# Forward substitution on GpSimd for the inverses of the 16x16 diagonal blocks

## The chip, the cores and the metric

The kernel runs on one core of one Trainium2 chip. The metric is the device time of one execution in microseconds (us); the median of several runs is compared.

## The reference

One block of a hybrid encoder on 256 frames of width 2048: a Mamba-2 SSD mixer and an RWKV-7 time mixer read the same normed input through one input projection, their outputs go through one output projection, and a SwiGLU feed-forward layer and a final norm follow. The part that matters here is the recurrence of the RWKV-7 mixer, over 32 heads of 64 channels:

```python
def step(S, inp):
    r_t, w_t, k_t, v_t, a_t, b_t = inp
    sa = jnp.einsum('bhvk,bhk->bhv', S, a_t)
    S = S * w_t[:, :, None, :] + sa[..., None] * b_t[:, :, None, :] + v_t[..., None] * k_t[:, :, None, :]
    return S, jnp.einsum('bhvk,bhk->bhv', S, r_t)
```

The kernel evaluates it in chunks of 64 frames. Within a chunk the vectors `sa` of its frames depend on each other through a triangular matrix with ones on its diagonal, so each chunk and head needs the inverse of one 64x64 unit triangular matrix.

## The kernel before

**Stages.** The work is a long row of weight products on TensorE. The weights are read in 512 KB pieces into `raw` (four buffers, issued by SyncE, whose queue is in order). Each piece is split into a high part `whi` by ScalarE (line 192) and a rest `wlo` by VectorE (line 193), four buffers each, and goes into three matmuls per tile: lines 277 to 279 in `gemm_a` (256 columns wide), lines 298 to 300 in `gemm_b` (512 wide). First comes the input projection of the RWKV columns, in eight windows of one pair of 128-channel blocks each (`ps_rkv`; four heads of 64 channels per window). Then come the columns of the SSD mixer (`ps_bc`, `ps_xs`, `ps_z`), the output projection in between (`ps_o`), and the feed-forward layer (`ps_gt`, `ps_up`, `ps_o`).

**Side work by ticks.** Each `gemm_a` or `gemm_b` calls `side.tick()` after every piece of weights. `Side` is a heap of functions with due times in ticks, counted from the start of a window; a function is called, and its instructions are emitted, at the first tick that is not before its due time. `window(pi, ticks)` fills the heap: `PREP` for pair pi, `AMATS` and `INV` for pair pi-1, `CHAIN` for pair pi-2. Windows 0 to 2 have 12 ticks (the 12 pieces of k, v and r), the others 16 (four more of the output projection), window 8 has 20 (the SSD's B and C columns). In windows of 12 ticks the due times of `INV` and `CHAIN` are scaled by 11.5/16. The compiler's order on each engine is fixed before the run. It is near the order of emission but not the same: in the trace, instructions of one chain on VectorE stand between those of others, and loads of weights that were emitted later stand ahead of an earlier transfer that is not yet ready.

**The inverse of one pair** (8 chunk slots of two heads each, so 16 matrices of 64x64, each with four 16x16 diagonal blocks, 64 small blocks in all):

- `inv_out` (lines 597 to 611) picks the diagonal blocks out of `atb` into `dg` on VectorE, sends them to DRAM (`sc_n`, line 604) and reads them back as `nb` (line 606), 64 partitions, one 16x16 block per partition, on SyncE's queue. GpSimd fills `xb` with unit matrices (lines 609 and 610).
- `inv_level(s)` for s = 1, 2, 4, 8 (lines 613 to 656) inverts the blocks in each partition by doubling: from inverses of size s to those of size 2s by two products X21 = X22 N21 X11. All of it is on VectorE: one copy (line 628), then ten products (line 650) and ten sums along the last axis (line 652).
- `inv_in` (lines 658 to 668) sends `xb` to DRAM (`sc_X`, line 660), reads it back as `cm` in the layout of 128 partitions (line 663), and makes `X` (line 666) and its transpose `XT` on VectorE.
- `lev16a`, `lev16b`, `lev32a`, `lev32b` (lines 684 to 717) go from 16 to 32 and 64 by small TensorE products `ps_b` (line 677), with steps on VectorE and ScalarE between them. The result `XF` is read by the chain of the next window (`step_r`, line 737).

`nb`, `xb`, `dg`, `X` and `XT` have one buffer each.

Of the kernel before, what the change touches and what calls it, by code (L numbers as in the profile page):

```python
# [13 lines left out]
ALU = mybir.AluOpType  # L14
AX = mybir.AxisListType
# [17 lines left out]

PREP = (1.081, 1.2, 4.2, 5.2, 5.536, 6.756, 8.05, 9.2)
AMATS = (0.132, 1.4, 2.027, 2.231, 2.69, 3.323, 6.493)
INV = (5.002, 6.276, 7.732, 9.62, 9.939, 11.691, 11.849, 12.652, 15.9)
STEPS = (0.667, 2.0, 5.0)
SSD = (0.9, 2.7, 4.842, 6.642, 8.442, 8.924, 10.724, 12.524, 12.657, 16.124)
CHAIN = (0.05, 1.043, 2.306, 3.569, 4.833, 5.933, 7.196, 8.459, 9.08, 11.159, 12.747, 13.38)
# [29 lines left out]
def tile_hybrid_block(ctx: ExitStack, tc: tile.TileContext, x, norm1_g, w_in, conv_w, conv_b, dt_bias, A_log, D_skip,  # L69
                      ssd_norm_g, mu, w0, w2, a0, a2, g2, k_k, k_a, r_k, gn_w, gn_b, w_out, norm2_g, w_gate, w_up,  # L70
                      w_down, norm_f_g, out):
    nc = tc.nc
    PS = bass.MemoryType.PSUM
    x = x[0]
    out = out[0]
# [10 lines left out]
    side = Side()  # L86
# [7 lines left out]
    def bc(ap, n):  # L94
        return ap.unsqueeze(ap.ndim).broadcast_to(list(ap.shape) + [n])
# [3 lines left out]
    xv = x.rearrange("(b p) d -> p b d", p=P)  # L99
# [52 lines left out]
    for hh in range(2):  # L152
        for s in range(2):
            m = mask2[hh * 64:(hh + 1) * 64, s]
# [4 lines left out]
    for s in range(2):  # L159
        for hh in range(2):  # L160
            a = hh * 64
# [48 lines left out]
    def finish(i, b):  # L210
        r = rstd[i][:, b:b + 1]
        nc.vector.tensor_reduce(r, ssq[i][:, b], axis=AX.X, op=ALU.add)
        nc.scalar.activation(r, r, AF.Sqrt, bias=eps6, scale=1.0 / D)
        nc.vector.reciprocal(r, r)
        return r
# [221 lines left out]
    def rwkv_pair(pi, st):  # L437
        cb0 = 2 * pi

        def tl(name, shape=(P, 2, T), bufs=1, tag=None):  # L440
            return rp.tile(list(shape), F32, name=name, tag=tag or name, bufs=bufs)
# [134 lines left out]
        def amat(name, key, half):  # L576
            def f():
                if half == 0:
                    st[name] = tl(name, (P, NCH, 2, 64), 2)
                dst = st[name]  # L580
                src = ch(st[key])
                ps = mxt("ps_a").rearrange("p (c t) -> p c t", c=4)
                for c in range(4):
                    for hh in range(2):
                        nc.tensor.matmul(hd(ps, hh)[:, c], hd(src, hh)[:, half * 4 + c],
                                         hd(st["ar"], hh)[:, half * 4 + c].rearrange("p a t -> p (a t)"),
                                         start=True, stop=True)
                nc.vector.tensor_tensor(dst[:, half * 4:half * 4 + 4].rearrange("p c a t -> p c (a t)"), ps,
                                        mask2.rearrange("p a t -> p (a t)").unsqueeze(1).broadcast_to([P, 4, P]),
                                        ALU.mult)  # L590
                if name == "atb":
                    d = dst[:, half * 4:half * 4 + 4, 0]
                    nc.vector.tensor_tensor(d, d, bc(st["nn"][:, half * 4:half * 4 + 4], 64), ALU.mult)
            return f


        def inv_out():
            tm = tl("t1", (P, NCH, 4, 16), 2)
            nc.vector.tensor_tensor(tm, st["atb"][:, :, 0].rearrange("p c (b t) -> p c b t", t=16),
                                    bc(bmask, 16).unsqueeze(1).broadcast_to([P, NCH, 4, 16]), ALU.mult)  # L600
            dg = tl("dg", (P, NCH, 16))
            nc.vector.tensor_reduce(dg, tm.rearrange("p c b t -> p c t b"), axis=AX.X, op=ALU.add)
            sc = dram.tile([NCH, P, 16], F32, name="sc_n")
            nc.sync.dma_start(out=sc.rearrange("c p t -> p c t"), in_=dg)
            nb = tl("nb", (64, 272))
            nc.sync.dma_start(out=nb[:, :256].rearrange("p (i t) -> p i t", t=16),
                              in_=sc.rearrange("c (x i) t -> (c x) i t", i=16))
            xb = tl("xb", (64, 272))
            nc.gpsimd.memset(xb, 0.0)
            nc.gpsimd.memset(xb[:, 0:256:17], 1.0)  # L610
            st["nb"], st["xb"] = nb, xb

        def inv_level(s):
            def f():
                nb, xb = st["nb"], st["xb"]
                nm = 8 // s

                def blocks(t, at, swap):

                    v = t[:, :nm * 34 * s].rearrange("p (m x) -> p m x", m=nm)[:, :, at:at + 16 * s]  # L620
                    v = v.rearrange("p m (j t) -> p m j t", t=16)[:, :, :, 0:s]
                    return v.rearrange("p m j t -> p m t j") if swap else v


                n21 = blocks(nb, s, False)
                x11 = blocks(xb, 0, True)
                if s == 1:
                    nc.vector.tensor_copy(blocks(xb, 16, False), n21)
                    return
                x22 = blocks(xb, 17 * s, False)  # L630
                x21 = blocks(xb, 16 * s, False)
                tt = tl("tt", (64, 64), 2)

                if s == 2:
                    cut = [(slice(0, nm), r) for r in range(s)]
                    shp = [64, nm, s, s]
                    tv = tt[:, :nm * s * s].rearrange("p (r m c) -> p m r c", r=s, c=s)
                else:
                    cut = [(m, slice(0, s)) for m in range(nm)]
                    shp = [64, s, s, s]  # L640
                    tv = tt[:, :nm * s * s].rearrange("p (m r c) -> p m r c", r=s, c=s)
                tj = tv.rearrange("p m j c -> p m c j")

                def product(out, a, b):

                    for m, r in cut:
                        pd = tl("pd", (64, 512), 2, tag="t1")
                        pv = pd[:, :shp[1] * s * s].rearrange("p (a c j) -> p a c j", c=s, j=s)
                        bb = b[:, m] if s == 2 else b[:, m].unsqueeze(1)
                        nc.vector.tensor_tensor(pv, a[:, m, r].unsqueeze(2).broadcast_to(shp), bb.broadcast_to(shp),  # L650
                                                ALU.mult)
                        nc.vector.tensor_reduce(out[:, m, r], pv, axis=AX.X, op=ALU.add)

                product(tv, n21.rearrange("p m j r -> p m r j"), x11)
                product(x21, x22, tj)
            return f

        def inv_in():
# [150 lines left out]
        def final():  # L809
# [3 lines left out]
            for j in range(2):  # L813
                for kk in range(2):
# [8 lines left out]
            nc.vector.tensor_tensor(yl, yo, yh.bitcast(F32), ALU.subtract)  # L823

        amats = [recept, sums, amat("atb", "bt", 0), amat("atb", "bt", 1), inv_out, amat("atk", "kt", 0),
                 amat("atk", "kt", 1)]
        inv = [inv_level(1), inv_level(2), inv_level(4), inv_level(8), inv_in, lev16a, lev16b, lev32a, lev32b]
        chain = [load2]
        for c in range(4):
            chain += [step_r(c), step_s(c)]  # L830
# [6 lines left out]
    def window(pi, ticks):  # L837
        if pi < 8:
            w = pairs[pi]
            w["load"]()  # L840
            for t, n in zip(PREP, ("decay", "rate", "keys", "keys2", "keysum", "btt", "vt", "ktt")):
                side.at(t, w[n])
        if 0 < pi < 9:
            w = pairs[pi - 1]
            for t, f in zip(AMATS, w["amats"]):
                side.at(t, f)
            for t, f in zip(INV, w["inv"]):
                side.at(t if ticks >= 16 else t * (ticks - 0.5) / 16, f)
        if pi > 1:
            for t, f in zip(CHAIN, pairs[pi - 2]["chain"]):  # L850
                side.at(t if ticks >= 16 else t * (ticks - 0.5) / 16, f)
# [5 lines left out]
    for pi in range(8):  # L857
        st = {}
        pairs.append(rwkv_pair(pi, st))
        window(pi, 16 if pi > 2 else 12)  # L860
        for i, (n, c) in enumerate((("k", CK), ("v", CV), ("r", CR))):
            ps = scaled(gemm_a(w_in, [(0, 256, c + pi * 256)], "ps_rkv"))
            t = pp.tile([P, 2, T], F32, name="rkv", tag="t" + n, bufs=1)
            for j in range(2):
                m = ((c - CR) // P) + 2 * pi + j
                shift(t[:, j], ps[:, j], omA[:, m:m + 1], colA[:, MU + m:MU + m + 1])
            st[n] = t
        out_rwkv(pi - 3)
        side.drain()


    window(8, 20)
    xzst = ExitStack()

# [6 lines left out]
    for i in range(4):  # L881
# [6 lines left out]
        for j in range(2):  # L888
            b = 2 * i + j
            conv(BC[:, b // 4, b % 4], ps[:, j], 16 + b)  # L890
    nc.scalar.activation(BC, BC, AF.Silu)
    out_rwkv(5)
    side.drain()
    window(9, 18)

    def ssd_group(g, xc, zs):
# [105 lines left out]
    for g in range(4):  # L1002
        xc = []
        for i in range(2):
            ps = scaled(gemm_a(w_in, [(0, 256, CXBC + g * 512 + i * 256)], "ps_xs"))
            t = xz.tile([P, 2, T], F32, name="xc", tag=f"xc{i}")
# [55 lines left out]
    for j in range(D_FF // 512):  # L1062
        c = j * 512
# [28 lines left out]
    for b in range(2):  # L1092
        s = slice(b * P, (b + 1) * P)
        for n, (hi, lo) in enumerate(ws):
# [5 lines left out]
            c = slice(n * 512, (n + 1) * 512)  # L1100
# [6 lines left out]
    for b in range(2):  # L1107
        r = finish(2, b)
        for n in (2, 3, 0, 1):
            c = slice(n * 512, (n + 1) * 512)  # L1110
            t = hg[b][n]
# [33 lines left out]
```

## Time and profile before

| what | value |
| --- | --- |
| median of 3 runs | 1673.48 us (1672.79 to 1674.52) |
| the profiled execution's own time | 1674.88 us |
| its span, first to last instruction | 1673.2 us |
| mean granted TensorE clock | 0.999 of full speed |
| busy: TensorE, weight loads, VectorE, ScalarE, GpSimd | 99%, 86%, 71%, 53%, 1% |

PE is TensorE, PEld its weight loads, DVE VectorE, ACT ScalarE, POOL GpSimd, SP SyncE; a q behind the name is the engine's sequencer or queue. In a row of instructions stand the line of the kernel, the engine, the operation, the tiles written and read (`out<-in`), their shapes and a count. In a timeline the first number is the start in us from the span's beginning, the second the length of the row, and the bracket behind it the idle time of the engine before it and who ended it. In the list of waits stand the total in us, the number of times and the longest.

### The profile page before, as it was taken

The page shows a single profiled execution, that of the slowest core. Times are in us where ns is not written, and L with a number is a line of the kernel's source. Part 1 is how long each engine was busy: PE and PEld are TensorE (multiplying, and loading weights), DVE is VectorE, ACT ScalarE, POOL GpSimd, SP SyncE. Part 2 cuts the span into 40 slices and gives each one's busy share as a digit, 9 for nine tenths or more (in the row PEclk, how much of TensorE's full clock was granted, in tenths as well). Part 3 has the DMA queues.
Part 4 walks back from the last instruction along what each step waited for, and adds up shares of the span by engine and source line. Part 5 has one row for each costly group of instructions (what it writes and reads, how often), then busy time and mean ns, then how long its engine had stood idle before and what let it go on. Part 6 is the DMA issues. An engine that isn't in the chain of part 4 may idle for free.

```text
span 1673.2 us, 30550 instructions
## 1 busy us (share of the span) xinstructions
PE 1654.7 (99%) x12386; PEld 1440.8 (86%) x12386; DVE 1196.1 (71%) x1859; ACT 892.7 (53%) x1390; POOL 18.0 (1%) x57
## 2 busy tenths in 40 slices
PE   8999999999999999999999999999999999999997
PEld 8999989899898998998988888888888888888886
DVE  7898889888888867978777746465565564554657
ACT  6655765765656456667565644444444444444444
POOL 3000000000000000000000000000000000000000
PEclk9999999999999999999999999999999999999999
DMA  8654445545455455665654666666666666666663
GB/s 256 173 147 117 131 127 147 145 121 148 119 150 146 121 171 182 204 209 157 177 171 152 204 192 190 194 190 189 191 190 197 186 193 191 189 189 197 190 190 126
DMA packets 212685, 286.91 MB, mean 171 GB/s; under 512 B 34978, under 2 KB 117696, under 8 KB 211904
## 3 DMA queue, kind: packets, MB, share of 16 engines
q1 hardware_dynamic: 211216, 282.67, 57.9%
q8 instruction: 97, 1.59, 0.4%
q0 software_dynamic: 752, 1.24, 0.3%
q10 hardware_dynamic: 576, 1.05, 0.2%
q14 instruction: 44, 0.36, 0.1%
HBM read 281.75 MB, written 3.18 MB: 170 GB/s over the span
## 4 chain that ended last, share of the span: by engine, by line
PE 73%; DVE 1%; DMA 0%; ACT 0%; issue 0%; DVEq 0%; SPq 0%
PE ps_o L298 8%; PE ps_o L300 7%; PE ps_o L299 7%; PE ps_gt L300 5%; PE ps_gt L298 5%; PE ps_up L299 5%; PE ps_gt L299 5%; PE ps_up L300 5%; PE ps_up L298 5%; PE ps_xs L277 2%; PE ps_xs L279 2%; PE ps_xs L278 2%; PE ps_z L300 2%; PE ps_z L299 2%; PE ps_z L298 2%; PE ps_bc L277 1%
## 5 line engine op out<-in xcount | busy, mean ns | idle before, releaser
L193 DVE TENSOR_TENSOR wlo<-raw,whi 128x1024 fp32r<-128x1024 f32 x508 | 620.2, 1221 | 373.9 <-ACT whi L192 372.2
L192 ACT CAST whi<-raw 128x1024 fp32r<-128x1024 f32 x508 | 532.9, 1050 | 623.5 <-PE ps_o L300 150.7
L277 PE MATMUL ps_rkv<-uh,whi 128*128 128x256 f32 x768 | 224.5, 292 | 0.0
L279 PE MATMUL ps_rkv<-uh,wlo 128*128 128x256 f32 x768 | 218.5, 285 | 0.7 <-DVE wlo L193 0.7
L278 PE MATMUL ps_rkv<-ul,whi 128*128 128x256 f32 x768 | 218.3, 284 | 0.0
L277 PEld LDWEIGHTS ps_rkv<-uh,whi 128*128 128x128 f32 x768 | 146.7, 191 | 5.5 <-issue 1.4
L279 PEld LDWEIGHTS ps_rkv<-uh,wlo 128*128 128x128 f32 x768 | 146.8, 191 | 1.7 <-DVE wlo L193 0.9
L278 PEld LDWEIGHTS ps_rkv<-ul,whi 128*128 128x128 f32 x768 | 146.8, 191 | 0.6
L298 PE MATMUL ps_gt<-whi,uh 128*128 128x512 f32 x352 | 137.1, 390 | 0.0
L299 PE MATMUL ps_gt<-wlo,uh 128*128 128x512 f32 x352 | 137.0, 389 | 0.0
L300 PE MATMUL ps_gt<-whi,ul 128*128 128x512 f32 x352 | 137.0, 389 | 0.0
L298 PE MATMUL ps_up<-whi,uh 128*128 128x512 f32 x352 | 136.9, 389 | 0.0
L299 PE MATMUL ps_up<-wlo,uh 128*128 128x512 f32 x352 | 136.9, 389 | 0.0
L300 PE MATMUL ps_up<-whi,ul 128*128 128x512 f32 x352 | 136.9, 389 | 0.0
L298 PE MATMUL ps_o<-whi,ah 128*128 128x512 f32 x336 | 131.7, 392 | 0.0
L300 PE MATMUL ps_o<-whi,al 128*128 128x512 f32 x336 | 130.9, 390 | 0.0
L299 PE MATMUL ps_o<-wlo,ah 128*128 128x512 f32 x336 | 130.7, 389 | 0.0
L311 DVE TENSOR_TENSOR h<-ps_o,h 128x512 f32<-128x512 f32 x184 | 120.0, 682 | 2.6 <-PE ps_o L300 2.2
L298 PE MATMUL ps_o<-whi,yh 128*128 128x512 f32 x256 | 105.7, 415 | 0.0
L299 PE MATMUL ps_o<-wlo,yh 128*128 128x512 f32 x256 | 100.2, 392 | 0.0
L300 PE MATMUL ps_o<-whi,yl 128*128 128x512 f32 x256 | 99.8, 394 | 0.0
L298 PEld LDWEIGHTS ps_up<-whi,uh 128*128 128x128 f32 x352 | 66.1, 188 | 13.7
(335 smaller groups left out, 3014.7 us busy)
## 6 DMA issues: line engine op xcount, KB each, us to landing
raw<-in_w_in_dram SPq DMA_DIRECT2D x180, 512.0 KB, 3.8
raw<-in_w_gate_dram SPq DMA_DIRECT2D x88, 512.0 KB, 3.8
raw<-in_w_up_dram SPq DMA_DIRECT2D x88, 512.0 KB, 3.7
raw<-in_w_down_dram SPq DMA_DIRECT2D x88, 512.0 KB, 4.6
raw<-in_w_out_dram SPq DMA_DIRECT2D x64, 512.0 KB, 4.4
csb<-cs_d SPq DMA_DIRECT2D x4, 1024.0 KB, 6.9
h<-in_x_dram SPq DMA_DIRECT2D x4, 512.0 KB, 7.5
g2s<-in_rwkv_g_dram SPq DMA_DIRECT2D x8, 256.0 KB, 3.5
```

The lines of the kernel that those rows point to most:

```text
L192: order(nc.scalar.copy(hi, raw))
L193: order(nc.vector.tensor_tensor(lo, raw, hi.bitcast(F32), ALU.subtract))
L277: nc.tensor.matmul(o, wh, uh[:, kt], start=first and b == 0, stop=False)
L278: nc.tensor.matmul(o, wh, ul[:, kt], start=False, stop=False)
L279: nc.tensor.matmul(o, wl, uh[:, kt], start=False, stop=last and b == 1)
L298: nc.tensor.matmul(ps[b], ah[:, s], hi[:, k], start=first, stop=False)
L299: nc.tensor.matmul(ps[b], ah[:, s], lo[:, k], start=False, stop=False)
L300: nc.tensor.matmul(ps[b], al[:, s], hi[:, k], start=False, stop=last)
L311: nc.vector.tensor_tensor(d, ps[b], d, ALU.add)
```

## The change

The four levels of doubling on VectorE go. In their place stands one function `inv_rows`, which inverts all 64 blocks by forward substitution on GpSimd: row i of the block, multiplied by the rows that are done, is added to all rows below it. Row 0 is a copy, rows 1 to 14 are a product and an addition each, 29 instructions of 64 partitions. All of them are handed out at due time 3.9. The send-back `inv_in` stays at 9.939, the levels behind it move. Windows of 12 ticks get a list of their own, `INV12`, where before the one list was scaled. `nb` and `xb` lose 16 unused columns, the scratch tile `pd` becomes 64x64 with a name of its own, `tt` goes.

```diff
-INV = (5.002, 6.276, 7.732, 9.62, 9.939, 11.691, 11.849, 12.652, 15.9)
+INV = (3.9, 9.939, 11.691, 12.3, 13.3, 15.9)
+INV12 = (3.9, 8.4, 9.9, 10.2, 10.9, 11.5)
...
-            nb = tl("nb", (64, 272))
+            nb = tl("nb", (64, 256))
...
-            xb = tl("xb", (64, 272))
+            xb = tl("xb", (64, 256))
...
-        def inv_level(s):
...
-                product(tv, n21.rearrange("p m j r -> p m r j"), x11)
-                product(x21, x22, tj)
+        def inv_rows(i0, i1):
+
+            def f():
+                nv = st["nb"][:, :256].rearrange("p (i t) -> p i t", t=16)
+                xv = st["xb"][:, :256].rearrange("p (t c) -> p t c", c=16)
+                for i in range(i0, i1):
+                    n, m = 15 - i, i + 1
+                    below = xv[:, m:, 0:m]
+                    if i == 0:
+                        nc.gpsimd.tensor_copy(below, nv[:, 0, 1:].unsqueeze(2))
+                        continue
+                    shp = [64, n, m]
+                    pd = tl("pd", (64, 64), 2)[:, :n * m].rearrange("p (t c) -> p t c", c=m)
+                    nc.gpsimd.tensor_tensor(pd, bc(nv[:, i, m:], m), xv[:, i, 0:m].unsqueeze(1).broadcast_to(shp),
+                                            ALU.mult)
+                    nc.gpsimd.tensor_tensor(below, below, pd, ALU.add)
             return f
...
-        inv = [inv_level(1), inv_level(2), inv_level(4), inv_level(8), inv_in, lev16a, lev16b, lev32a, lev32b]
+        inv = [inv_rows(0, 15), inv_in, lev16a, lev16b, lev32a, lev32b]
...
-            for t, f in zip(INV, w["inv"]):
-                side.at(t if ticks >= 16 else t * (ticks - 0.5) / 16, f)
+            for t, f in zip(INV if ticks >= 16 else INV12, w["inv"]):
+                side.at(t, f)
```

More of the change, by code (lines that the diff above doesn't have):

```diff
@@ L611, in inv_out @@
             st["nb"], st["xb"] = nb, xb
-        def inv_level(s):
+        def inv_rows(i0, i1):
             def f():
[L615 to L652, printed above, removed]
-                product(tv, n21.rearrange("p m j r -> p m r j"), x11)
-                product(x21, x22, tj)
```

## The prediction

> **What bounds the kernel now.** I read the page's busy shares and the chain that ended last, then the windows by stage, then what TensorE waited for, and last the timelines around one pair's inverse.
>
> ```profile
> span 1673.2 us, 30550 instructions
> PE 1654.7 (99%) x12386; PEld 1440.8 (86%) x12386; DVE 1196.1 (71%) x1859; ACT 892.7 (53%) x1390; POOL 18.0 (1%) x57
> PE 73%; DVE 1%; DMA 0%; ACT 0%; issue 0%; DVEq 0%; SPq 0%
> ```
> ```profile
> 0.00:650.00 650.00, 640.79 (x7493) 588.73 (x7494) 556.12 (x1065) 394.34 (x792) 17.46 (x56) 1.00 0.53 147
> 650.00:1673.00 1023.00, 1013.94 (x4895) 852.07 (x4893) 640.03 (x795) 498.36 (x599) 0.54 (x1) 1.00 0.62 187
> ```
>
> TensorE (PE) is busy 99% of the span and is nearly all of the chain. The columns of the windows are length, then busy time of PE, PEld, DVE, ACT and POOL, then the granted clock. The change lives in the first 650 us, where the eight RWKV pairs are worked. There VectorE (DVE) is busy 556.12 of 650 us, 86%, and GpSimd (POOL) 17.46, but TensorE still lacks only 650.00 - 640.79 = 9.2 us. A busy engine that is late shows as a wait of the one that needs it, so the waits of PE say what a lighter VectorE can return:
>
> ```profile
> PE ps_w L737 <- ACT rs L733: 1.8, 2, 1.0
> PE ps_R L225 <- DVE diag_r L224: 1.7, 1, 1.7
> PE ps_n L247 <- DMA h<-in_x_dram: 1.6, 1, 1.6
> PE ps_up L114 <- DVE eps L105: 1.1, 1, 1.1
> PE ps_b L677 <- DVE t1s L690: 0.8, 1, 0.8
> PE ps_b L677 <- DVE X L666: 0.8, 2, 0.4
> PE ps_rkv L279 <- DVE wlo L193: 0.7, 1, 0.7
> PE ps_dt L396 <- DVE dt_c L377: 0.6, 1, 0.6
> ```
>
> These eight are 9.1 us, the whole lack. Four belong to the start (L225, L247, L114, L396, 5.0 us), which the change does not touch. The four that can be touched are 1.8 + 0.8 + 0.8 + 0.7 = 4.1 us, 0.25% of the span. That caps what faster supply of TensorE can give.
>
> **What is removed.** Per pair, one copy and twenty small VectorE instructions (products L650, sums L652) leave.
>
> ```profile
> 0.00:650.00 650.00, 45.00 (x160) 1.00 0.53 147
> L628 DVE COPY xb<-nb x8: 155/168/169, 99.0 to 546.8; 64x8 f32<-64x8 f32 x8
> ```
>
> The first row is the first 650 us with the instructions on tile pd alone: 160 of them, 45.00 us of VectorE. With 8 copies of 0.168 us that is 46.3 us, 5.8 us per pair. On VectorE that is a saving; on TensorE it is worth only the waits above. I credit the 0.8 us of X (below: in the two short windows the send-back and its consumer are re-timed) and the 0.8 us of t1s. The other 2.5 us I leave: the ps_w waits end on ScalarE, and the wlo wait is a single one. Sum so far -1.6 us.
>
> **What is added on GpSimd.** Row 0 is one copy, rows 1 to 14 a product and an addition each: 29 instructions per pair, of (15-i)(i+1) elements per partition, 15 to 64 and 665 over the 14 rows, so 47.5 on average, each depending on the one before. No two-input GpSimd instruction is in this trace. The nearest rows:
>
> ```profile
> 12.31 1.04 POOL L148 TENSOR_SCALAR_AFFINE_SELECT trimask<-trimask 128x128 f32<-128x128 f32 x1
> 13.31 1.38 POOL L155 TENSOR_SCALAR_AFFINE_SELECT mask<-mask 64x64 f32<-64x64 f32 x4
> ...
> 113.32 0.32 POOL L609 MEMSET xb<- 64x272 f32 x1 [32.01 <-DVE wlo L193]
> 113.69 0.12 POOL L610 MEMSET xb<- 64x16 f32 x1
> ```
>
> Nearest in size and kind (reads, writes, 64 elements) is L155: four in 1.38 us, 0.345 us each. Between two dependent memsets lie 113.69 - 113.32 - 0.32 = 0.05 us. I take 0.40 us per instruction, a chain of 29 x 0.40 = 11.6 us. Ends: as cheap as the 64x16 memset, 0.17 each, 4.9 us; as dear as the 128-element select, 1.09 each, 31.6 us. POOL has nothing else to do in that time.
>
> [...] No row here shows a two-input GpSimd instruction.
>
> **How long the chain may be.** A late chain meets three others in turn. One is SyncE's (SP's) queue, which sends xb back in order (L660) with the weight loads behind it. The second is VectorE's order, in which X (L666) stands ahead of weight splits (wlo, L193). The third is TensorE's order, where ps_b (L677) stands between weight matmuls. The seventh pair, in a full window, rows of four engines in order of time:
>
> ```profile
> 475.62 0.48 SPq L606 DMA_DIRECT2D nb<-sc_n  x1
> 478.89 0.17 DVE L628 COPY xb<-nb 64x8 f32<-64x8 f32 x1 [0.24 <-DMA nb<-sc_n]
> 483.34 8.08 SPq L290 DMA_DIRECT2D raw<-in_w_out_dram  x3
> 493.30 0.64 DVE L652 TENSOR_REDUCE xb<-pd 64x64 f32<-64x512 f32 x1
> 494.01 0.49 SPq L660 DMA_DIRECT2D sc_X<-xb  x1
> 496.39 0.47 SPq L663 DMA_DIRECT2D cm<-sc_X  x1
> 500.70 0.43 DVE L666 TENSOR_TENSOR X<-cm,pmask 128x256 f32<-128x256 f32 x1
> 502.04 1.21 DVE L193 TENSOR_TENSOR wlo<-raw,whi 128x1024 fp32r<-128x1024 f32 x1
> 505.43 0.28 PE L278 MATMUL ps_rkv<-ul,whi 128*128 128x256 f32 x1
> 505.55 0.28 PE L279 MATMUL ps_rkv<-uh,wlo 128*128 128x256 f32 x1
> 505.76 0.22 PE L677 MATMUL ps_b<-X,atb 32*32 32x32 f32 x2
> ```
> ```profile
> SPq L660 <- DVE xb L652: 18.6, 8, 2.9
> ```
>
> The chain starts at 478.89 and ends at 493.94, 15.05 us, most of it VectorE's other work in between. SP is free at 491.42 and already waits for it, 2.3 us a pair on average (18.6 over 8) without harm: the loads behind it fill raw buffers that are needed later. X is done at 501.13 and TensorE reads it at 505.76, 4.6 us later. So a GpSimd chain of 11.6 us is 3.4 us early; SP would wait from 12.5 us; the ps_b on TensorE waits from 15.05 + 4.63 = 19.7 us. That is 0.68 us per instruction. The weight splits behind X on VectorE have cover of their own: with four buffers each of raw, whi and wlo they run ticks ahead of TensorE.
>
> The other end is the first inverse, in a window of 12 ticks:
>
> ```profile
> 98.99 0.17 DVE L628 COPY xb<-nb 64x8 f32<-64x8 f32 x1
> 110.51 0.66 DVE L652 TENSOR_REDUCE xb<-pd 64x64 f32<-64x512 f32 x1
> 117.86 0.43 DVE L666 TENSOR_TENSOR X<-cm,pmask 128x256 f32<-128x256 f32 x1 [0.49 <-DMA cm<-sc_X]
> 118.43 0.54 PE L677 MATMUL ps_b<-X,atb 32*32 32x32 f32 x23 [0.39 <-DVE X L666]
> ```
>
> The chain took 111.17 - 98.99 = 12.2 us with no slack at TensorE. Here the change re-times the steps: the old list was scaled by 11.5/16, which put inv_in at 7.14 and lev16a at 8.40 (ticks 8 and 9); INV12 has 8.4 and 9.9 (ticks 9 and 10), a tick later. A tick of gemm_a is 24 matmuls at 505.55 - 505.43 = 0.12 us, so at least 2.9 us. The budget becomes 12.2 + 0.1 + 2.9 = 15.2 us or more, 0.52 us per instruction. The chain of 11.6 fits, and the 0.8 us of waits for X (these two windows) goes.
>
> **What is moved, priced at nothing.** The send-back and its return are the same two DMAs in the same queue, the round trip unchanged. lev16b goes from tick 12 to 13 and lev32a from 13 to 14 in full windows; lev32b stays at 16. In the short windows lev16b and lev32a now fall into one tick (10.2 and 10.9, tick 11), which has to hold the addition to XT and its transposition between them; if nothing hides these, TensorE waits for two VectorE steps of X's size, 0.43 us each, 0.9 us a window in two windows. The new steps can split or merge groups of side matmuls. One group costs the entry 505.76 - 505.55 against 0.12, plus as much on leaving, about 0.2 us; one more or less in each of eight windows is 1.6 us, of either sign. That both signs are open is why I take zero.
>
> **Sum.** -1.6 us on the profiled span of 1673.2 us; that execution took 1674.88 us, the median of the three timed runs is 1673.48. On the median: 1671.9 us, -0.1%. A change under 0.2%, 3.3 us, I call none, about what this kernel's measurement can tell.
>
> **Rival: GpSimd too slow, TensorE waits (slower).** One mechanism: each GpSimd instruction takes over the budget. At 0.70 us the chain is 20.3 us. In the five full windows TensorE loses 20.3 - 19.7 = 0.6 us each, in the two short ones 5.1 each, and the last window taken like a full one. Sum 13.8 us, less the 1.6: 1685.7 us. It decides from 0.52 us per instruction. What could bring it there are VectorE's long two-input instructions:
>
> ```profile
> L193 DVE TENSOR_TENSOR wlo<-raw,whi 128x1024 fp32r<-128x1024 f32 x161 | 195.5, 1215 | 19.3 <-ACT whi L192 18.0
> ```
>
> wlo runs 195.5 of the 650 us, 30%. If each GpSimd read that meets one waits out half of 1.215 us, that adds 0.30 x 0.61 = 0.18 us, 0.58 each and 16.8 us in all: within the full windows' 19.7, 1.6 us over in the two short ones, so 1673.48 - 1.6 + 3.2 = 1675.1, no change still. If every one waits so, 1.01 each, 29.3 us: 9.6 x 6 + 14.1 x 2 = 85.8 us, 1757.7. [...] Chance of slower, all together, 0.19.
>
> **Rival: the lighter VectorE pays fully (faster).** All 4.1 us of waits go, and side groups merge, one less per window: 4.1 + 1.6 = 5.7 us, 1667.8 us. For it speaks the 86% of VectorE; against it that two of the waits end on ScalarE. Chance 0.16.
>
> **Rival: nothing changes because SP still waits.** With the chain at 15 us the SP wait stays as it was and only the waits for X go: 1672.7. It falls within no change, whose chance is 0.65 together.
>
> **How the numbers follow.** Forecast 1671.9; its own range, one group per window and the waits either way, 1669.5 to 1675.5. Toward slower the range reaches to 1682.0, past the shared-read case and most of the way to 0.70 us; below 1669.5 and above 1682.0 I leave about 0.08 and 0.11. Faster 0.16, same 0.65, slower 0.19.
>
> **What would show it.** VectorE down about 46 us in the first 650 us, GpSimd up by 29 instructions a pair, start to start near 0.4 us; sc_X issued no later after nb lands than 15 us; no wait of PE for X; PE idle in that stretch between 5 and 9 us. I am wrong if start to start on GpSimd exceeds 0.52 us and PE waits for X in most windows, or if the wlo instructions get visibly longer than 1.215 us while GpSimd runs.

## The result and the profile after

The changed kernel took 1756.78 us (median of 4 runs, 1752.63 to 1760.03) against 1673.81 us before (median of 4 runs, 1672.79 to 1674.52): ratio 1.0495, 95% interval 1.0471 to 1.0519. The forecast was no change. The profiled execution took 1752.63 us. Its page, span and busy shares:

```profile
span 1750.9 us, 30571 instructions
PE 1674.9 (96%) x12386; PEld 1459.6 (83%) x12386; DVE 1158.2 (66%) x1691; ACT 891.6 (51%) x1390; POOL 103.5 (6%) x289
```

The span is 77.7 us longer. TensorE's idle time went from 1673.2 - 1654.7 = 18.5 us to 1750.9 - 1674.9 = 76.0 us, 57.5 us more, and its busy time rose by 20.2 us although it executes the same 12386 matmuls. The first part is named by what TensorE waited for:

```profile
PE ps_r L705 <- DVE sn L736: 36.0, 6, 6.6
PE ps_rkv L280 <- DVE wlo L194: 7.8, 4, 2.2
PE ps_b L652 <- ACT Y L772: 6.0, 1, 6.0
PE ps_b L652 <- DVE X L641: 5.9, 1, 5.9
PE ps_b L652 <- DVE X L646: 1.8, 2, 1.3
PE ps_bc L280 <- DVE wlo L194: 1.7, 1, 1.7
```

The rows of `sn`, `wlo` and `ps_b` are 36.0 + 9.5 + 13.7 = 59.2 us; before, waits of these kinds were 0 + 0.7 + 1.6 us. The largest is new: six waits of about 6 us for `sn`, the running state of the recurrence, which the change does not touch (`step_s` of the pair one earlier; in this kernel lines 735 and 736, before 760 and 761). The timeline of the seventh pair, VectorE (DVE) and TensorE (PE) in order of time, shows why:

```profile
475.08 0.33 PE L701 MATMUL ps_r<-vt,atk 64*64 64x64 f32 x4
...
479.07 0.43 DVE L641 TENSOR_TENSOR X<-cm,pmask 128x256 f32<-128x256 f32 x1 [8.84 <-DMA cm<-sc_X]
479.53 0.45 DVE L646 STREAM_TRANSPOSE XT<-X 128x256 f32<-128x256 f32 x1
479.90 0.67 DVE L232 TENSOR_TENSOR ps_rkv<-ps_rkv,R 128x512 f32<-128x512 f32 x1
480.48 0.69 DVE L562 STREAM_TRANSPOSE btt<-bt 128x512 f32<-128x512 f32 x1
481.09 0.25 DVE L735 TENSOR_TENSOR sn<-ps_s,sn 128x128 f32<-128x128 f32 x1
...
481.65 0.28 DVE L736 TENSOR_TENSOR sn<-sn,pt 128x128 f32<-128x128 f32 x1
...
481.98 0.48 PE L705 MATMUL ps_r<-sn,ar 64*64 64x64 f32 x4 [6.57 <-DVE sn L736]
```

`X` waits 8.84 us for `cm`, and VectorE runs nothing else in that time. Behind `X` stand its own transposition, a scaling, another transposition and `sn`; on TensorE the matmul that reads `sn` is next in its order, and it stands still for 6.57 us. In the kernel before, the same two instructions began 8 to 9 us ahead of `X`, which began at 500.70:

```profile
491.71 0.25 DVE L760 TENSOR_TENSOR sn<-ps_s,sn 128x128 f32<-128x128 f32 x1
492.48 0.27 DVE L761 TENSOR_TENSOR sn<-sn,pt 128x128 f32<-128x128 f32 x1
```

So `X` has moved forward in VectorE's fixed order, past `sn`. Two rows of the stretch from 80 to 660 us add up what stood still beside TensorE: VectorE's eight waits for `cm`, and the waits of SyncE (SP) for the result of GpSimd (POOL):

```profile
DVE X L641 <- DMA cm<-sc_X: 67.9, 8, 9.1
```
```profile
SPq L635 <- POOL xb L630: 87.3, 8, 12.5
```

The 20.2 us of extra busy time come with a lower granted clock. Windows of this kernel around that stall (length, then busy time of PE, PEld, DVE, ACT and POOL, then the granted clock, the DMA engines' share and GB/s):

```profile
475.00:481.90 6.90, 0.42 (x6) 0.20 (x4) 2.79 (x8) 1.26 (x4) 0.42 (x2) 0.75 0.61 162
481.90:488.50 6.60, 6.42 (x41) 5.90 (x42) 4.17 (x7) 2.56 (x6) 0.00 (x0) 0.50 0.44 120
488.50:495.00 6.50, 6.50 (x71) 6.30 (x70) 2.50 (x4) 3.56 (x17) 0.00 (x0) 0.98 0.31 86
```

In the 6.6 us behind the stall the clock was 0.50, and 41 matmuls ran where 71 did afterwards. Behind each of the six waits for `sn` (4.90 to 6.57 us) the next 3.4 us have a clock of 0.50. The page's row of the clock (40 slices, tenths of full speed) shows the dips in the first third of the span. The mean is 0.977; before, it was 0.999:

```profile
PEclk9999989899998999999999999999999999999999
```

### The profile page after: what moved, and what is told of

Read it like the earlier page. It is cut to its first block, busy times and chain, and to the rows that moved or that the text cites. A ratio compares the mean times of both kernels' runs of the same rounds, so it can differ in the third digit from the quotient of the medians.

```text
span 1750.9 us, 30571 instructions
## 1 busy us (share of the span) xinstructions
PE 1674.9 (96%) x12386; PEld 1459.6 (83%) x12386; DVE 1158.2 (66%) x1691; ACT 891.6 (51%) x1390; POOL 103.5 (6%) x289
## 4 chain that ended last, share of the span: by engine, by line
PE 63%; DVE 0%; ACT 0%; DVEq 0%; issue 0%
PE ps_o L299 7%; PE ps_o L301 7%; PE ps_o L300 7%; PE ps_gt L299 5%; PE ps_gt L300 5%; PE ps_up L300 5%; PE ps_gt L301 5%; PE ps_up L299 5%; PE ps_up L301 5%; PE ps_xs L278 2%; PE ps_xs L280 2%; PE ps_xs L279 2%; PE ps_z L301 2%; PE ps_z L299 2%; PE ps_z L300 2%; PE ps_yd L923 1%
## 5 line engine op out<-in xcount | busy, mean ns | idle before, releaser
L278 PE MATMUL ps_rkv<-uh,whi 128*128 128x256 f32 x768 | 233.4, 304 | 0.0
L280 PE MATMUL ps_rkv<-uh,wlo 128*128 128x256 f32 x768 | 224.2, 292 | 7.8 <-DVE wlo L194 7.8
L279 PE MATMUL ps_rkv<-ul,whi 128*128 128x256 f32 x768 | 224.7, 293 | 0.0
L280 PEld LDWEIGHTS ps_rkv<-uh,wlo 128*128 128x128 f32 x768 | 153.9, 200 | 8.4 <-DVE wlo L194 8.3
L278 PEld LDWEIGHTS ps_rkv<-uh,whi 128*128 128x128 f32 x768 | 153.9, 200 | 6.2 <-issue 1.4
L279 PEld LDWEIGHTS ps_rkv<-ul,whi 128*128 128x128 f32 x768 | 154.3, 201 | 0.6
L299 PEld LDWEIGHTS ps_up<-whi,uh 128*128 128x128 f32 x352 | 66.1, 188 | 13.7
```

Source lines behind the costliest of these rows:

```text
L278: nc.tensor.matmul(o, wh, uh[:, kt], start=first and b == 0, stop=False)
L279: nc.tensor.matmul(o, wh, ul[:, kt], start=False, stop=False)
L280: nc.tensor.matmul(o, wl, uh[:, kt], start=False, stop=last and b == 1)
L299: nc.tensor.matmul(ps[b], ah[:, s], hi[:, k], start=first, stop=False)
```

## The experiments

The diffs below are abridged, and the comments in them belong to this text. Each run's ratio is to runs of the kernel before that were taken beside it (medians 1673.75 to 1674.45 us).

Three theories stood at the start. **A**: `X` stands too early in VectorE's order, `sn` and then TensorE wait behind it, and the clock halves after each of these stalls (0.50 in the windows above). **B**: SP's queue is at fault, which holds the weight loads behind the send-back of `xb`. **C**: GpSimd and VectorE disturb each other through shared reads.

**X later in VectorE's order.** `inv_in` is cut in two; the second part, `X` and `XT`, gets due times of its own and is held on VectorE behind the last `ws` (or shift) handed out before it.

```diff
-INV = (3.9, 9.939, 11.691, 12.3, 13.3, 15.9)
-INV12 = (3.9, 8.4, 9.9, 10.2, 10.9, 11.5)
+INV = (3.9, 9.939, 10.9, 11.691, 12.3, 13.3, 15.9)
+INV12 = (3.9, 8.4, 8.9, 9.9, 10.2, 10.9, 11.5)
...
+        def inv_x():
+            with tc.issue_after(gate["ins"]):      # last ws or shift on VectorE
+                X ...; turn("XT", "X")
```

> The changed kernel, with one thing altered: X (and its transpose) is held on VectorE's queue behind the last ws of the chain (in the first windows behind the last shift), where it stood before the change. Theory A (order): GpSimd's chain of about 13 us is longer than the order on VectorE allows for, X stands in front of sn, VectorE waits there 8 us for cm, TensorE waits 6 us for sn and then runs some us at half clock. Then the sn waits of TensorE (36 us) and most of the half clock go: 1675 to 1695 us. Theory B (SyncE's queue): xb's transfer holds the weight loads behind it for 11 us and that costs the time. Then it stays above 1735 us. Theory C (shared reads): GpSimd's two-input instructions slow VectorE's. Then it also stays above 1735 us.

Measured: 1693.87 us (1692.88 to 1697.02), ratio to before 1.0121, interval 1.0106 to 1.0136. That is 62.9 of the 83.0 us, with GpSimd's work, the ticks of the rows and the place of the small transfers in SP's queue as in the changed kernel. No wait for `sn` is left, VectorE's waits for `cm` fell from 67.9 to 17.4 us. What TensorE still waited for, the two longest rows:

```profile
PE ps_rkv L280 <- DVE wlo L194: 7.0, 4, 1.9
PE ps_b L658 <- DVE X L647: 6.8, 1, 6.8
```

**The two small DMAs on GpSimd's queue** (theory B).

```diff
-            nc.sync.dma_start(out=sc.rearrange(...), in_=st["xb"]...)
+            nc.gpsimd.dma_start(out=sc.rearrange(...), in_=st["xb"]...)
...
-            nc.sync.dma_start(out=cm, in_=sc.rearrange(...))
+            nc.gpsimd.dma_start(out=cm, in_=sc.rearrange(...))
```

> The changed kernel with the send-back sc_X and its return cm issued on GpSimd's queue in place of SyncE's; X stays where it stands on VectorE. Theory A: the waits for sn stay, only the waits for wlo that come from late weight loads (9.5 us) and a little half clock go: 1735 to 1755 us. Theory B: no load waits behind xb any more, below 1700 us. Theory C: unchanged, 1750 to 1760 us.

Measured: 1750.13 us (1748.69 to 1753.10), ratio 1.0456, interval 1.0441 to 1.0472. SP no longer waits for `xb`, and TensorE's waits for `sn` are the same:

```profile
PE ps_r L705 <- DVE sn L736: 35.9, 6, 6.7
```

Theory B, which asked for less than 1700 us, falls: taking SP's 87.3 us of waiting away gave 6.7 of the 83.0 us. The time fits theory A, at the edge C too. One part of A's forecast missed: the waits for `wlo` were to go, and they stayed at 8.4 + 1.5 us.

**Both edits together.**

> X held late on VectorE and both transfers on GpSimd's queue. Theory A with a small share of B: 5 to 15 us below the run with X late alone, 1670 to 1680 us, near the kernel before. Theory C: above 1735 us.

Measured: 1698.17 us (1695.35 to 1698.96), ratio 1.0145, interval 1.0128 to 1.0162. The further gain of 5 to 15 us that was expected over X held back alone (1693.87) did not come.

**The kernel before, with the same GpSimd work beside it** (theory C): per pair one copy and 28 two-input instructions that read `nb` and scratch tiles and write scratch tiles that no result needs; the inverse stays on VectorE.

```diff
+        def rows_idle():                           # called with the first level
+            nc.gpsimd.tensor_tensor(pd, bc(nv[:, i, m:], m), nv[:, i, 0:m]..., ALU.mult)
+            nc.gpsimd.tensor_tensor(v, v, pd, ALU.add)
```

> The kernel before, doubling on VectorE as it was, with the same number and sizes of GpSimd instructions per pair added on scratch tiles that nothing reads (a copy and 28 two-input instructions, contiguous outputs). It prices GpSimd's work and its effect on VectorE alone. Theory A: the work itself is nearly free, 1673 to 1680 us. Theory C: most of the 83 us appear here too, above 1720 us; wlo's mean length grows.

Measured: 1674.42 us (1673.58 to 1676.49), ratio 1.0007, interval 0.9998 to 1.0016. The two engines' rows in this kernel:

```profile
L627 POOL TENSOR_TENSOR xs<-xs,pq 64x28 f32<-64x28 f32 (+3 forms) x112 | 63.5, 567 | 8.8
L193 DVE TENSOR_TENSOR wlo<-raw,whi x508: 1172/1225/1343, 8.4 to 1643.6; 128x1024 fp32r<-128x1024 f32 x170
```

GpSimd's instructions are slowed, the additions to 0.567 us on average; `wlo` keeps its median of 1.225 us, and VectorE's busy time rises by only 2.8 us (1196.1 to 1198.9). The time stays. Theory C falls.

**X held behind sn only.** As in the first experiment, but the hold is on the last pending `sn` instead of `ws`.

> X and XT are a part of their own again, held on VectorE only behind the pending update of the state, sn, and not behind what follows. Theory A (X stands too early in VectorE's order, so that sn waits behind it and TensorE behind sn): TensorE's six waits for sn of 36.0 us go, with the half-clock stretches behind them, though VectorE goes on waiting for cm; the time lands within 8 us of the kernel that holds X behind ws, 1690 to 1705 us. Rival, that the loss comes from VectorE standing idle at X as such (67.9 us of waits for cm) and not from sn alone: still above 1720 us.

Measured: 1715.15 us (1709.06 to 1719.03), ratio 1.0239, interval 1.0221 to 1.0257: between the two expectations, so theory A's forecast of 1690 to 1705 missed here. The waits for `sn` are gone, and the next one in the chain takes their place:

```profile
PE ps_y L752 <- DVE ws L721: 9.7, 5, 2.4
```

VectorE's waits for `cm` (34.0 us) now delay `ws` (here line 721), which stood next behind `X`. So not `sn` alone: every instruction behind the waiting `X` that TensorE soon needs is late, and `sn` was the dearest: holding `X` behind `sn` gave 41.6 us, holding it behind `ws` as well another 21.3.

**The same substitution on VectorE.** Only the engine of the 29 instructions is changed; ticks as in the changed kernel.

```diff
-                    nc.gpsimd.tensor_tensor(pd, ...)      # and the copy, and the addition
+                    nc.vector.tensor_tensor(pd, ...)
```

> The forward substitution with the changed kernel's ticks, but its 29 instructions a pair run on VectorE instead of GpSimd. Theory A: the order on VectorE is made with times of VectorE's own instructions, so X stands where cm has landed and sn does not wait; the half-clock stretches go, and the time comes to 1673 to 1682 us, VectorE's busy time to 1158 plus some 50 us. Rival T, that the changed tick lists (all rows at 3.9, the send-back at 9.9 or 8.4) are at fault whatever the engine: above 1700 us, with TensorE waits for sn of some 6 us.

Measured: 1684.74 us (1683.64 to 1686.90), ratio 1.0063, interval 1.0050 to 1.0076: 2.7 us over the top of what theory A expected, far under rival T. `X` stands behind `sn` and `ws` again (in one window `sn` at 427.60 us, `ws` at 432.13, `X` at 439.11). The time left is mostly one kind of wait, and SP's list beside it shows where it comes from:

```profile
PE ps_rkv L280 <- DVE wlo L194: 7.9, 4, 2.8
PE ps_b L652 <- DVE X L641: 2.3, 1, 2.3
```
```profile
SPq L469 <- DVE rkv L355: 36.1, 5, 7.2
```

Line 469 loads the weights of the group norm into tiles that are not free yet: the group norm of the pair before still reads them. In the five full windows it stood in SP's order behind four of the next window's weight loads before, and behind three since the change; for 7.2 us each window no weight is loaded. One window of the kernel before, and one of the changed kernel:

```profile
428.61 17.59 SPq L264 DMA_DIRECT2D raw<-in_w_in_dram  x4
448.83 1.30 SPq L468 DMA_DIRECT2D gnw<-in_rwkv_gn_w_dram  x2
```
```profile
485.93 13.25 SPq L265 DMA_DIRECT2D raw<-in_w_in_dram  x3
506.01 0.63 SPq L469 DMA_DIRECT2D gnw<-in_rwkv_gn_w_dram  x1
```

**The group norm's loads held back**, with the substitution on VectorE: five weight loads go ahead of them.

```diff
-CHAIN = (0.05, ...
+CHAIN = (5.0, ...
...
+            with tc.issue_after(gate["raw"]):      # last weight load issued so far
+                load2_()
```

> The forward substitution on VectorE with the changed ticks, and the group norm's loads held back so that five of the next window's weight loads stand ahead of them on SP (three before). Theory A with SP's order as the cause of TensorE's waits for wlo (9.8 us in five, and half clock behind three of them): these waits go and the time falls from 1684.7 by 8 to 14 us to 1671 to 1677. Rival, that the wlo waits come from VectorE's own load or order: 1682 us or more.

Measured: 1673.59 us (1671.68 to 1674.03), ratio 0.9993, interval 0.9984 to 1.0002. As expected, 11.1 us less. SP's row is gone, and the waits for `wlo` are down to 2.3 + 0.6 us, none longer than 0.6 us.

**TensorE kept busy during the stall.** The changed kernel with 52 more matmuls of 128x256 ahead of the one that waits for `sn`, in pairs 1 to 6, into a bank that nothing reads; the matmuls that read `sn` are held behind them.

```diff
+                    if c == 3 and j == 0 and 0 < pi < 7:
+                        for _ in range(52):
+                            nc.tensor.matmul(fill[:, :T], uh[:, 0, 0:P], uh[:, 1], start=True, stop=True)
```

> The changed kernel, with 52 additional matmuls of 128x256 into a bank of their own (0.12 us each, 6.2 us a pair) set ahead of the matmul that waits for sn, in pairs 1 to 6; their result is not used. They do work that no output needs, in the time in which TensorE stood idle. Theory A with the half clock coming from the stall itself: the six stalls are filled, the half-clock stretches behind them (about 15 to 20 us lost in all) go, and the kernel is faster though it does more: 1735 to 1748 us. Rival, that the half clock comes from load and not from the stall, or that the filling shifts the wait: 1755 to 1775 us.

Measured: 1754.48 us (1753.18 to 1760.36), ratio 1.0485, interval 1.0467 to 1.0503; expected were 1735 to 1748, so this part of the forecast missed. The seventh pair, the 30 us around it, and TensorE's busy time over the whole kernel:

```profile
477.95 6.50 PE L706 MATMUL ps_fill<-uh 128*128 128x256 f32 x52
```
```profile
470.00:500.00 30.00, 29.26 (x342) 27.15 (x338) 15.93 (x27) 13.35 (x37) 4.77 (x15) 1.00 0.34 93
```
```profile
PE 1705.8 (97%) x12698; PEld 1491.2 (85%) x12698; DVE 1158.7 (66%) x1691; ACT 892.4 (51%) x1390; POOL 104.4 (6%) x289
```

With the stall filled the clock stayed at 1.00 where it had been 0.50, so in the seventh pair the lower clock came with the stall and not with the load. Over the whole kernel TensorE did 312 x 0.12 = 37.4 us more work in the same time. Its busy time rose by only 30.9 us over the changed kernel, so 6.5 of the 20.2 us of slower matmuls are gone; the mean clock is 0.987 after 0.977. Its idle time fell to 47.7 us: the waits for `sn` are down to 1.4 us, but others grew (`wlo` 10.6 + 1.8 us, `ps_w` 5.8 us), and the mean clock stays below the 0.999 of before. So the price of these stalls is shown in the seventh pair; as a whole the run does not separate it.

**Three repairs together, substitution on GpSimd.** X held behind `ws`, the group norm's loads behind five weight loads, and the `ps_b` products held behind the last wide matmuls handed out before them. That hold is meant for the first `ps_b` of the short windows, whose four levels come at ticks 11.9 to 11.96, but it stands on every `ps_b` product of every window.

> X held behind the last ws, and the two waits mended that were left in that kernel: the group norm's loads are handed out later (5.0 for 0.05), so that five of the next window's weight loads stand ahead of them on SP, and in the first short window the matmuls that take X are held behind the last wide gemm's. Theory A with these two as all that is left of the loss: no TensorE wait over 1.5 us between 100 and 640 us, no half clock there, 1670 to 1680 us; if VectorE's 46 us of relief were worth anything, below 1672.5. Rival, that something else of the change costs time (GpSimd beside VectorE, say): 1690 us or more.

Measured: 1687.68 us (1684.58 to 1692.57), ratio 1.0079, interval 1.0066 to 1.0092: between the two expectations, so theory A's 1670 to 1680 us missed. In the profile's windows (same columns as above) the loss sits in the short windows alone:

```profile
100.00:220.00 120.00, 109.89 (x1458) 103.56 (x1457) 87.71 (x149) 67.25 (x136) 26.13 (x67) 0.94 0.46 124
220.00:650.00 430.00, 427.05 (x5214) 387.19 (x5213) 341.81 (x567) 254.03 (x520) 66.54 (x185) 1.00 0.49 139
```
```profile
PE ps_b L666 <- DVE t1s L679: 8.1, 2, 5.1
```

The same two windows of the kernel before:

```profile
100.00:220.00 120.00, 118.51 (x1609) 111.40 (x1609) 107.94 (x218) 71.98 (x146) 1.12 (x6) 1.00 0.49 133
220.00:650.00 430.00, 427.40 (x5123) 385.47 (x5122) 365.87 (x674) 257.76 (x536) 2.67 (x14) 1.00 0.50 139
```

From 220 to 650 us TensorE is idle for 2.95 us, before for 2.60. From 100 to 220 us it lacks 10.1 us, before 1.5. The repair of the short windows moved the wait from `X` to `t1s` (line 679): 8.1 us there, and 1.0 us left for `X`.

**Short windows as before, full windows with GpSimd.** The first two pairs keep the doubling on VectorE and its ticks; the other six have the forward substitution on GpSimd and the repairs of the run before: `X` behind `ws`, the group norm's loads held back (in all eight pairs), and the hold on the `ps_b` products.

```diff
+        rows = [inv_rows(0, 15)] if pi > 1 else [inv_level(1), inv_level(2), inv_level(4), inv_level(8)]
```

> The first two pairs (short windows) keep the four doubling levels on VectorE with the ticks of the kernel before; the other six have the forward substitution on GpSimd, X held behind the last ws and the group norm's loads behind five weight loads. In the kernel with all three repairs the full windows took 68.2 us each, as before (68.0), and 12 us were lost in the short windows, behind t1s. Theory A (that is all that is left of the loss): 1671 to 1677 us, no TensorE wait over 1.5 us between 100 and 640 us. If the 35 us that VectorE no longer works in the six full windows bought anything: 1671 or less. Rival, that GpSimd beside VectorE still costs in the full windows: 1680 us or more.

Measured: 1674.38 us (1673.15 to 1675.96), ratio 1.0001, interval 0.9992 to 1.0010: theory A's number. Page, and SP's waits for GpSimd:

```profile
PE 1653.8 (99%) x12386; PEld 1440.8 (86%) x12386; DVE 1168.0 (70%) x1733; ACT 891.3 (53%) x1390; POOL 82.8 (5%) x231
```
```profile
SPq L685 <- POOL xb L680: 66.6, 6, 12.6
```

Six pairs of the substitution run on GpSimd, SP waits 11.1 us for each, VectorE is 28 us lighter than before, TensorE's longest wait past 100 us is 0.9 us, and the time is that of before. So the steps add up: 62.9 us for `X` in VectorE's order (1756.8 to 1693.9), 6.2 us for SP's order with the hold on `ps_b` (to 1687.7), 13.3 us for putting the short windows back as they were (to 1674.4). The split between the last two is not clean, since the kernel of 1687.7 changed both at once; SP's order by itself was worth 11.1 us on VectorE.

## Why the prediction was wrong

- **What was removed was of the right order, and no run beat the cap.** VectorE fell by 37.9 us (1196.1 to 1158.2) where 46.3 were counted. The 46.3 us are the sum of rows that overlap their neighbours: in the kernel before, the row that starts at 491.07 for 0.71 us ends 0.07 us after the start of the next, at 491.71. About 0.05 us on each of the 168 rows would make up the difference; that is an estimate. A lighter VectorE brought TensorE nothing: 1674.38 and 1673.59 us are the best that any version reached, and neither differs from before.
- **GpSimd's cost was right within 15%.** The eight chains took 11.7 to 13.3 us where 11.6 were forecast. The seventh pair's, quoted in part:

```profile
460.54 1.07 POOL L624 COPY xb<-nb 64x15 f32<-64x15 f32 x1 [24.44 <-DMA nb<-sc_n]
463.32 0.28 POOL L630 TENSOR_TENSOR xb<-xb,pd 64x48 f32<-64x48 f32 x1
463.45 1.23 DVE L194 TENSOR_TENSOR wlo<-raw,whi 128x1024 fp32r<-128x1024 f32 x1 [0.56 <-ACT whi L193]
463.68 1.14 POOL L628 TENSOR_TENSOR pd<-nb,xb 64x55 f32<-64x55 f32 x1
...
473.22 0.21 POOL L630 TENSOR_TENSOR xb<-xb,pd 64x15 f32<-64x15 f32 x1
```

  From 460.54 to 473.43 us are 12.9 us, 0.445 us per instruction where 0.40 was taken, under both limits named (0.52 and 0.68). Undisturbed, start to start is 0.36 us (463.32 to 463.68). The rival's mechanism is there: the product at 463.68 met `wlo` and took 1.14 us; one of the same shape, at 470.24, took 0.27. Over the eight chains 30 of the 224 products and additions took 0.54 to 1.36 us, 21 of them beside a `wlo`, and the other 194 at most 0.36 us. GpSimd paid nearly all of it: `wlo` kept its median of 1.225 us, and its longest went from 1.228 to 1.328 us. And with the doubling still on VectorE the same GpSimd work cost no time (1674.42 us).
- **The number of the dearest rival is luck.** For a chain of 29.3 us the prediction gave 1757.7 us, within 1 us of the 1756.78 measured. That every instruction waits and takes 1.01 us, no run shows: the chain took 12.9 us, 0.445 us per instruction, and the time was lost in other waits.
- **The step that failed first: "How long the chain may be".** The budget of 19.7 us was measured at TensorE's `ps_b`, the reader of `X`, with every order as it was. But the order on each engine is made anew when the kernel is compiled: `X` had begun 9 us behind the first `sn` instruction, and now its turn came ahead of it, where `cm` had not landed. In the full windows `X` is not late for its reader, the question was what is queued behind it on VectorE. The text named the weight splits there, which have cover, and not the step `sn`, which has none. Cost: 62.9 of 83.0 us, by the run that moved `X` back.
- **The second step that failed: the short windows.** The step "a tick later, at least 2.9 us" read the new due times as a later place of `ps_b` on TensorE. In the first short window the chain ran from 98.82 to 112.06 us, 13.2 us against a budget of 15.2, and `X` began at 117.75, as before (117.86). But TensorE stood at `ps_b` from 112.46 us on, where it had come at 118.04 before. `lev16a` comes at a later tick, yet its matmuls do not stand later. In the second short window TensorE waited 6.01 us for `t1s`, which in VectorE's order now stood behind the group norm's `Y` (186.40 us); before, it had stood ahead of it (`t1s` at 169.36, `Y` at 174.00). The changed kernel's rows:

```profile
117.75 0.43 DVE L641 TENSOR_TENSOR X<-cm,pmask 128x256 f32<-128x256 f32 x1 [9.05 <-DMA cm<-sc_X]
118.32 1.74 PE L652 MATMUL ps_b<-X,atb 32*32 32x32 f32 x64 [5.86 <-DVE X L641]
187.20 0.42 DVE L665 TENSOR_TENSOR t1s<-ps_b,msk 128x256 f32<-128x256 f32 x1
187.76 1.08 PE L652 MATMUL ps_b<-XT,t1s 32*32 32x32 f32 x64 [6.01 <-ACT Y L772]
```

  Cost: about 13 us, taken from the run that put these windows back, against one that had their levels at other ticks.
- **Priced at nothing, and not nothing: the moves in SP's queue.** "The send-back and its return are the same two DMAs in the same queue" holds, and taking SP's longer wait for `xb` away gave 6.7 us, and nothing once `X` was held back. But the group norm's loads moved one weight load forward, which makes TensorE wait for `wlo` (9.5 us here). With the substitution on VectorE, where they stood likewise, holding them back was worth 11.1 us.
- **Not in any rival: the price of a stall.** The sums took a wait for its own length. TensorE's busy time rose by 20.2 us with the same 12386 matmuls, and the windows show the half clock behind the stalls (0.50 in the 3.4 us behind each of the eight waits of 4.9 us or more between 80 and 660 us).

Why the compiler placed `X` so early was not shown and stays open. With the same ticks and the substitution on VectorE it stood behind `sn`, so with these ticks it hangs on the engine of the rows; that the compiler takes GpSimd's chain for shorter than it is would explain it, but no run measures that.

## What to carry to other kernels

When a chain is moved to another engine, ask what stands behind its consumer on the consumer's engine, and treat that order as open: here it was made anew with the change, in the DMA queue too. Pin the consumer behind what must not wait for it, and check in the trace that it stands there. And price a stall of TensorE above its own length, since here a clock of 0.50 followed each of the eight waits of 4.9 us or more.

## What the hardware showed

Stalls of TensorE of some 2 us were at times followed by half the clock, and at times not. In the kernel with the substitution on VectorE, the first of these two waits was not followed by a slow stretch, the second was (below them the windows behind each, with the clock):

```profile
177.88 1.11 PE L652 MATMUL ps_b<-X,atb 32*32 32x32 f32 x64 [2.33 <-DVE X L641]
534.35 0.39 PE L280 MATMUL ps_bc<-uh,wlo 128*128 128x256 f32 x1 [1.88 <-DVE wlo L194]
```
```profile
177.90:181.30 3.40, 3.40 (x140) 3.18 (x141) 3.19 (x8) 2.59 (x6) 0.00 (x0) 1.00 0.03 5
535.30:538.70 3.40, 3.40 (x19) 3.18 (x19) 2.65 (x3) 0.20 (x1) 0.00 (x0) 0.50 0.87 210
```

So a wait of 1.88 us was followed by a clock of 0.50, and a longer one of 2.33 us by 1.00. In the changed kernel the 3.4 us behind the six waits of 1.28 to 2.17 us between 80 and 660 us had 0.66 (after 2.17 us), 0.57 (after 1.86 us) and four times 1.00 (after 1.98, 1.74, 1.65 and 1.28 us). What decides it was not shown. GpSimd's two-input instructions of 15 to 64 elements per partition took 0.21 to 0.32 us undisturbed, which no row of the kernel before had shown.
